# Side work, operand sums and first heads re-ordered in a pipelined attention sweep

## The chip, the cores and the metric

The kernel runs on one core of one Trainium2 chip. The core has five engines with queues of their own: TensorE (PE, matmuls; PEld is its weight load), VectorE (DVE), ScalarE (ACT), GpSimd (POOL) and SyncE (SP, which here only issues DMAs). ACT and POOL issue some DMAs too. Each engine works through its instructions in the order in which they were written into its queue. The metric is the device time of one launch in microseconds (us); lower is better.

## What is computed

One layer of an encoder is applied to two groups of requests, g = 0 and 1, each of 512 tokens of width 1024, with shared weights; all arrays are fp32. A mLSTM branch and an attention branch start from one normalized input and are merged by gates; then come an output projection, a feed-forward block, a gated embedding and a last norm. The change lies in the attention branch. Cut to that:

```
qa = (rmsnorm(c_q, g_q) @ w_uq).reshape(B, S, 8, 128 + 64)
q_nope, q_rope = qa[..., :128], rope(qa[..., 128:], cos, sin)
kv = (rmsnorm(c_kv, g_kv) @ w_ukv).reshape(B, S, 8, 128 + 128)
k_nope, va = kv[..., :128], kv[..., 128:]
k_rope = rope(k_r, cos, sin)
s = q_nope @ k_nope^T + q_rope @ k_rope^T        # per head
p = softmax(s * (128 + 64) ** -0.5)
y_a = (p @ va) @ w_ao
x = x + (g_m * y_m + g_a * y_a) @ w_out          # y_m = (...) @ w_mo, mLSTM branch
```

## The kernel before

**Precision.** An fp32 product is made of three passes on PE: each operand is split into a part rounded for PE ("hi", a cast on ACT) and the rest ("lo", a subtraction on DVE, `lo_of`), and hi·hi, hi·lo and lo·hi are added in PSUM. So each operand costs ACT one instruction and DVE one. The tiles are 128 partitions by 512.

**Order.** Up to the attention sweep, and behind it, the compiler's scheduler simulates the engines and may re-order instructions that do not depend on each other. Within the sweep (`pinned[0]` true, L1121 to L1207) the instructions of PE, ACT, DVE and POOL stand in the order of the source. SP's queue is not pinned, and work written behind the sweep may still be placed among the sweep's.

**Before the sweep** (L701 to L1120). Sixteen merge gates keep PE busy up to 604.8 us. Then come: the split of the latents `lat` (ckv, then cq); the projection of all values (L712: two halves, each 2 groups x 4 blocks x 6 matmuls, written to DRAM as `vd`); the keys' rotary part `kst` (L741: a load `gs`, `rope_steps`, casts `kh`, lo parts `kl`); weights of heads 0 and 1 (`wa_load`, `wa_split`); for head 0 the rotary queries (`rot_proj`, six steps of `rot` on DVE, `rot_hi` on ACT, `rot_lo` on DVE, for both groups), keys and queries (`proj_hi`, `proj_lo`); and the rotary projection of heads 2 and 3, group 0 (`rot_proj(1, 0)`). `rot_proj(m, g)` makes the rotary part for heads 2m and 2m + 1.

**The sweep** (L1122) runs over 17 units u; u = 2 x head + group for 16 of them, and the last only finishes. Four units are a block: m = u // 4, r = u % 4. A unit u does, in this order:

- `score(u, 0)`, `expo(u, 0)`, `score(u, 1)`: five matmuls into a bank, the row maximum on DVE (`mx`), the exponent on ACT (`p`), which also sums the row (`den`);
- the last transposes of the unit before, `turn(u - 1, 3)`: four on PE (`pt`), the hi cast `aph` on ACT, the lo part `apl` on DVE; and the reciprocal `rc` of its row sums on DVE;
- the keys of the next unit (`proj_hi(kn, ...)`, `pj` to `qh`, `ql`), the values' split (`vh` on ACT, `vl` on POOL);
- `sums_row(u - 1)`: `rc` is transposed on PE, copied by ACT into `rb` (one buffer), stored by a DMA of POOL (`rsd`) and read back by another DMA of POOL, spread over 128 partitions;
- **side work**: the operands P1, P2 (r = 1), P7 (r = 2) and P6 (r = 3) of the next stage (`hop_hi`: the sum for P7 on DVE and for P6 on POOL, and the hi casts), and some rotary steps;
- `weigh(u - 1)`: twelve matmuls p · v into `av`; `weighed(u - 1)`: ACT copies it (`oz`), POOL multiplies it by `rb`, and a DMA stores it;
- `turn(u, 0)`, `score(u, 2)`, `turn(u, 1)`, `expo(u, 2)`; then side work again: the weight splits of a later head (r = 1 and 3) and the lo parts of the operands (`los`);
- the queries of the next unit, `score(u, 3)`, `turn(u, 2)`, `expo(u, 3)`; and a `rot_proj` (r = 0 and 3).

At u = 12 the rotary tiles give way to weight tiles of the next stage, and at u = 14 the latents to sixteen tiles X2, into which its operands are then loaded.

**Behind the sweep** two products by 7-multiplication blocks (`chain`, `Seven`, `Ops`) apply w_mo and w_ao. Their operands are sums of quarters, `P1` to `Q4` (`Ops.part`); the sums of the first product, P5 and Q4, are POOL's (L916, L922, L923), and so are most sums of its weights (L975 to L985).

Of the kernel before, what the change touches and what calls it, by code (L numbers as in the profile page):

```python
# [7 lines left out]
F32 = mybir.dt.float32  # L8
F32R = mybir.dt.float32r
# [6 lines left out]
P = 128  # L16
T = 512
NB = T // P
G = 2
# [43 lines left out]
def encoder_kernel(ctx: ExitStack, tc: tile.TileContext, a):  # L63
# [89 lines left out]
    def lo_of(out, src, hi, e=V):  # L153
        e.tensor_tensor(out=out, in0=src, in1=hi.bitcast(F32), op=ALU.subtract)  # L154
# [546 lines left out]
    Q = Slots("Q", vt=2, rb=1, qkv=12, qst=4, p=3, ph=1, pl=1)  # L701
    QL = Slots("QL", lat=16)
    lat = {}
    for n in ("ckv", "cq"):
        lat[n] = [[split(early[f"{n}{i}", g], QL, "lat", n) for i in range(2)] for g in range(G)]

    LAT.close()
# [1 line left out]


    vd = [[dr.tile([NB, P, T], F32, name=f"vd{g}{i}") for i in range(2)] for g in range(G)]
    for half in range(2):  # L712
        whi, wlo = weight(a["wv"][half])
        for g in range(G):
            for i in range(NB):
                bk = bank()
                for k in range(2):
                    n = slice(T * k, T * k + T)
                    hi, lo = (x[:, i * P : (i + 1) * P] for x in lat["ckv"][g][k])
                    E.matmul(bk, hi, whi[:, n], start=k == 0, stop=False)  # L720
                    E.matmul(bk, lo, whi[:, n], start=False, stop=False)
                    E.matmul(bk, hi, wlo[:, n], start=False, stop=k == 1)
# [18 lines left out]
    kst = []  # L741
    for g in range(G):
        gs = AX("rt", "gs")
        nc.sync.dma_start(gs[0:64], gsd[g])
        for _ in rope_steps(gs, AX("rt", "rs"), 2):
            pass
        kh = Q.pool.tile([P, T], F32R, name=f"kh{g}")
        kl = Q.pool.tile([P, T], F32R, name=f"kl{g}")
        for o in (0, 64):
            S.copy(kh[o : o + 64], gs[0:64])  # L750
        for o in (0, 64):
            V.tensor_tensor(out=kl[o : o + 64], in0=gs[0:64], in1=kh[0:64].bitcast(F32), op=ALU.subtract)
        kst.append((kh, kl))

    halves_ = [(hd, g) for hd in range(AH) for g in range(G)]
    NU = len(halves_)
    was, wload, qn, kn, vn, vts, rots, rsteps, qst, att = ({} for _ in range(10))
# [2 lines left out]
        wload[hd] = WP("wst", "wst", F32, (P, 1024))  # L760
        nc.sync.dma_start(wload[hd][:, 0:768], a["wa"][hd])

    def wa_split(hd):
        w = was[hd] = [WP(n, n, F32R, (P, 1024)) for n in ("whi", "wlo")]
        st = wload[hd]
        for c in (slice(256, 768), slice(0, 256)):
            if c.start == 256 or hd in (0, 1, 3, 5):
                S.copy(w[0][:, c], st[:, c])  # L768
                lo_of(w[1][:, c], st[:, c], w[0][:, c])

    def rot_proj(m, g):
        t = rots[m, g] = AX("rt", "rp")
# [319 lines left out]
        srcs = [a["w8"][W8[f"{kind}{i}"]] for i in (c, c + 4)]  # L1092
        return ops, lambda: Seven(srcs, 4, ops, outputs(put), e)

    for hd in range(2):
        wa_load(hd)
        wa_split(hd)
    v_load(0)
    for g in range(G):
        rot_proj(0, g)  # L1100
        rot(0, g, 6)
        rot_hi(0, g)
        rot_lo(0, g)
# [9 lines left out]
    def hop_hi(n, k):  # L1113
        src = hops.part(n, k)
# [3 lines left out]
        return lo, src, hi  # L1118

    hop_load(0)  # L1120
    pinned[0] = True  # L1121
    for u in range(NU + 1):  # L1122
        now, then, nxt = u < NU, u > 0, u + 1 < NU
        m, r = u // 4, u % 4
        if now:
            score(u, 0)
            expo(u, 0)
            score(u, 1)
        if nxt:
            v_load(u + 1)  # L1130
            if r == 0 and m < 3:
                wa_load(2 * m + 2)
            if r == 2 and m < 3:
# [23 lines left out]
        if r == 0 and 0 < m < 4:  # L1157
            rot_hi(m, 1)
            rot_lo(m, 1)
        if m < 3:  # L1160
            if r == 0:
                rot(m + 1, 0, 2)
            if r == 1:
                rot(m + 1, 0, 4)
            if r == 2:
                rot(m + 1, 1, 4)
            if r == 3:
                rot(m + 1, 1, 2)
                rot_hi(m + 1, 0)
                rot_lo(m + 1, 0)  # L1170
# [10 lines left out]
        if r == 1 and m < 3:  # L1181
            wa_split(2 * m + 2)
        if r == 3 and m < 3:
            wa_split(2 * m + 3)
# [12 lines left out]
        if r == 0 and m < 3:  # L1197
# [473 lines left out]
```

## Time and profile before

| what | us |
|---|---|
| three timed runs | 1920.03, 1922.84, 1924.75 (median 1922.84) |
| the profiled execution | 1919.33 |
| its span, first to last instruction | 1917.5 |
| mean granted clock of PE, full speed 1 | 0.985 |
| value projection begins | 604.80 |
| first score matmul | 638.97 |
| first matmul of the next product | 896.16 |

In a row of the timeline stand the start, the length, the engine, the line (all work of the sweep has L79, the helper that pins it, so one goes by names), the operation, out<-in, and in brackets the idle time before it with what ended it. In the table of windows each engine has its busy time and count, then come the granted clock, the DMA engines' share and GB/s. A matmul of 512 columns shows as 0.39 us, but the next starts 0.23 us behind it. A unit is named below by the start of its window.

### The profile page before, as it was taken

How to read it: one execution, taken by the hardware profiler on the slowest of the kernel's cores; microseconds unless marked ns; L12 is line 12 of the kernel's file. 1: busy time of each engine (PE TensorE's matmuls, PEld its weight loads, DVE VectorE, ACT ScalarE, POOL GpSimd, SP SyncE). 2: the span in 40 equal slices, each digit the busy share in tenths (PEclk: the TensorE clock that was granted, in tenths of full speed). 3: DMA queues.
4: the chain of work that ended last, by engine and by line, in shares of the span. 5: the costliest groups of instructions: out<-in, count | busy, mean ns of one | idle time of the engine just before them, and what ended most of it. 6: DMA issues, size and time to landing. Idle time of an engine off the chain costs nothing.

```text
span 1917.5 us, 24414 instructions
## 1 busy us (share of the span) xinstructions
PE 1843.9 (96%) x8817; PEld 1528.6 (80%) x8817; DVE 1240.7 (65%) x2078; ACT 870.7 (45%) x1705; POOL 423.5 (22%) x329
## 2 busy tenths in 40 slices
PE   9999999999999888986999999999999999999997
PEld 7889898988888666764878888888888887878786
DVE  6757576776521777764698578444444469878756
ACT  6355556563323565564353346433333345434432
POOL 0000000100000122245142002566646623011000
PEclk9999999999999999998999999999999999999998
DMA  4211112212324223235664432323222347533242
GB/s 171 62 56 56 66 45 68 65 45 94 121 93 153 87 80 89 78 100 195 211 217 162 134 127 102 105 88 129 94 102 89 116 143 237 169 125 106 95 142 94
DMA packets 102024, 216.10 MB, mean 113 GB/s; under 512 B 11536, under 2 KB 22224, under 8 KB 101904
## 3 DMA queue, kind: packets, MB, share of 16 engines
q1 hardware_dynamic: 87456, 165.49, 25.7%
q10 hardware_dynamic: 12096, 43.00, 6.9%
q0 software_dynamic: 2352, 6.07, 1.1%
q8 instruction: 69, 1.13, 0.3%
q14 instruction: 51, 0.42, 0.1%
HBM read 160.24 MB, written 54.26 MB: 112 GB/s over the span
## 4 chain that ended last, share of the span: by engine, by line
PE 81%; DVE 10%; DMA 3%; ACT 3%; issue 2%; POOL 1%; SPq 0%; ACTq 0%; DVEq 0%; POOLq 0%
PE b L1004 12%; PE b L1006 12%; PE b L1005 12%; PE mm L183 8%; PE mm L185 8%; PE mm L184 8%; PE mm L79 3%; PE nm L622 3%; PE sc L79 2%; PE pj L79 2%; PE mm L542 2%; PE mm L541 2%; PE mm L540 2%; DVE xl L154 1%; PE pt L79 1%
## 5 line engine op out<-in xcount | busy, mean ns | idle before, releaser
L1004 PE MATMUL b<-xh,wp 128*128 128x512 f32 x1148 | 441.4, 392 | 7.2 <-ACT u L1045 2.3
L1005 PE MATMUL b<-xl,wp 128*128 128x512 f32 x1148 | 447.3, 391 | 1.0 <-DVE xl L154 1.0
L1006 PE MATMUL b<-xh,wp 128*128 128x512 f32 x1148 | 443.4, 391 | 0.7 <-DVE wp L154 0.7
L948 ACT CAST wp<-wst 128x512 fp32r<-128x512 f32 (+1 forms) x270 | 164.6, 612 | 303.1 <-PE b L1006 242.5
L154 DVE TENSOR_TENSOR wp<-wst,wp 128x512 fp32r<-128x512 f32 (+1 forms) x270 | 231.6, 860 | 70.0 <-ACT wp L948 69.8
L1004 PEld LDWEIGHTS b<-xh,wp 128*128 128x128 f32 x1148 | 215.5, 188 | 59.4 <-ACT wp L948 6.1
L1005 PEld LDWEIGHTS b<-xl,wp 128*128 128x128 f32 x1148 | 215.5, 188 | 48.3 <-DVE xl L154 2.0
L1006 PEld LDWEIGHTS b<-xh,wp 128*128 128x128 f32 x1148 | 215.5, 188 | 48.2 <-DVE wp L154 1.6
L183 PE MATMUL mm<-hh,whi 128*128 128x512 f32 x560 | 219.3, 392 | 0.0
L184 PE MATMUL mm<-hl,whi 128*128 128x512 f32 x560 | 218.9, 391 | 0.0
L185 PE MATMUL mm<-hh,wlo 128*128 128x512 f32 x560 | 218.8, 391 | 0.0
L1050 DVE TENSOR_TENSOR u<-b,u 128x512 f32<-128x512 f32 x90 | 61.7, 689 | 132.4 <-PE b L1006 82.6
L185 PEld LDWEIGHTS mm<-hh,wlo 128*128 128x128 f32 x560 | 105.4, 188 | 22.0 <-DVE wlo L154 0.3
L183 PEld LDWEIGHTS mm<-hh,whi 128*128 128x128 f32 x560 | 105.6, 189 | 21.6 <-DVE to L382 0.2
L184 PEld LDWEIGHTS mm<-hl,whi 128*128 128x128 f32 x560 | 105.5, 188 | 21.5
L975 POOL TENSOR_TENSOR s<-wst,wst 128x512 f32<-128x512 f32 (+1 forms) x30 | 48.7, 1624 | 319.6 <-DMA wst<-wd 137.5
L168 ACT CAST whi<-wst 128x1024 fp32r<-128x1024 f32 x61 | 64.1, 1051 | 109.5 <-PE mm L184 70.4
L1361 POOL TENSOR_TENSOR sg<-sg,u 128x512 f32<-128x512 f32 x30 | 55.0, 1834 | 204.1 <-DVE u L1050 204.1
L154 DVE TENSOR_TENSOR wlo<-wst,whi 128x1024 fp32r<-128x1024 f32 (+1 forms) x65 | 77.7, 1198 | 34.5 <-ACT whi L768 19.6
L1045 ACT COPY u<-b 128x512 f32<-128x512 f32 x90 | 50.8, 589 | 96.7 <-PE b L1006 69.2
L79 POOL TENSOR_TENSOR vl<-avt,vh 128x512 fp32r<-128x512 f32 x16 | 21.1, 1320 | 307.5 <-ACT vh L79 307.5
L154 DVE TENSOR_TENSOR xl<-ld,xh 128x512 fp32r<-128x512 f32 x105 | 79.2, 785 | 5.0 <-ACT xh L932 4.4
(369 smaller groups left out, 3642.3 us busy)
## 6 DMA issues: line engine op xcount, KB each, us to landing
wst<-w SPq DMA_DIRECT2D x73, 512.0 KB, 3.4
wst<-w ACTq DMA_DIRECT2D x60, 512.0 KB, 3.6
ld<-actd SPq DMA_DIRECT2D x77, 256.0 KB, 3.5
actd<-t SPq DMA_DIRECT2D x40, 256.0 KB, 2.8
x<-x SPq DMA_DIRECT2D x32, 256.0 KB, 4.2
ld<-hzd SPq DMA_DIRECT2D x32, 256.0 KB, 4.3
wst<-wd ACTq DMA_DIRECT2D x16, 512.0 KB, 3.9
actd<-sg SPq DMA_DIRECT2D x30, 256.0 KB, 2.0
```

Of the source, the lines that this page charges most:

```text
L79: r = f(*args, **kw)
L154: e.tensor_tensor(out=out, in0=src, in1=hi.bitcast(F32), op=ALU.subtract)
L168: S.copy(hi[:, :n], st[:, :n])
L183: E.matmul(bk, whi[:, c], hi, start=k == 0, stop=False)
L184: E.matmul(bk, whi[:, c], lo, start=False, stop=False)
L185: last_mm[0] = E.matmul(bk, wlo[:, c], hi, start=False, stop=k == nk - 1)
L622: E.matmul(bk, l, r, start=n == 0, stop=n == len(terms) - 1)
L948: S.copy(hi, src)
L1004: E.matmul(bk, whi[:, c], hi, start=bool(first) and k == 0, stop=False, **sk)
L1005: E.matmul(bk, whi[:, c], lo, start=False, stop=False, **sk)
L1006: E.matmul(bk, wlo[:, c], hi, start=False, stop=k == self.kh - 1, **sk)
L1050: V.tensor_tensor(out=t, in0=b, in1=t, op=ALU.add if name == "P2" else ALU.subtract)
```

## The change

It re-orders; no arithmetic is added or taken away.

1. Before the sweep: cq is split ahead of ckv; head 0's weights, rotary queries, keys and queries and then the keys' rotary part come ahead of the value projection; the values' weights are split into tiles of the pool H in place of the weight pool; head 1's weights are loaded between the two halves and split within unit 0; `rot_proj(1, 0)` moves to the end of unit 0.
2. P6's sum is done at the very start of the units with r = 3, on POOL for m < 3 and on DVE for m = 3; its cast stays where it was, its lo part moves to the next unit.
3. The other side work of DVE and ACT is put singly or by twos between other instructions: P1's and P2's casts ahead of the first exponent, the rotary steps in five places, weight casts and lo parts apart, the lo parts of the operands behind the unit's last lo part. The operands' loads come at r = 0.

```diff
-    for n in ("ckv", "cq"):
+    for n in ("cq", "ckv"):
...
-    for half in range(2):
-        whi, wlo = weight(a["wv"][half])
+    def v_proj(half):
+        st = WP("wst", "wst", F32, (P, 1024))
+        nc.sync.dma_start(st, a["wv"][half])
+        w = [split(st[:, k * T : (k + 1) * T], H, "h", "wv") for k in range(2)]
         for g in range(G):
...
-    def wa_split(hd):
-        w = was[hd] = [WP(n, n, F32R, (P, 1024)) for n in ("whi", "wlo")]
-        st = wload[hd]
-        for c in (slice(256, 768), slice(0, 256)):
-            if c.start == 256 or hd in (0, 1, 3, 5):
-                S.copy(w[0][:, c], st[:, c])
-                lo_of(w[1][:, c], st[:, c], w[0][:, c])
+    QK, RO = slice(256, 768), slice(0, 256)
+    def wa_hi(hd, c):
+        if hd not in was:
+            was[hd] = [WP(n, n, F32R, (P, 1024)) for n in ("whi", "wlo")]
+        S.copy(was[hd][0][:, c], wload[hd][:, c])
+    def wa_lo(hd, c):
+        hi, lo = was[hd]
+        lo_of(lo[:, c], wload[hd][:, c], hi[:, c])
...
-    for hd in range(2):
-        wa_load(hd)
-        wa_split(hd)
-    v_load(0)
+    wa_load(0)
+    wa_split(0, RO)
+    wa_split(0, QK)
     for g in range(G):
         rot_proj(0, g)
+    for to, n, off in ((kn, "ckv", 512), (qn, "cq", 256)):
+        proj_hi(to, 0, n, off)
+        proj_lo(to, 0)
+    for g in range(G):
         rot(0, g, 6)
         rot_hi(0, g)
         rot_lo(0, g)
-    for to, n, off in ((kn, "ckv", 512), (qn, "cq", 256)):
-        proj_hi(to, 0, n, off)
-        proj_lo(to, 0)
-    rot_proj(1, 0)
+    kst = []
...
+    v_proj(0)
+    wa_load(1)
+    v_proj(1)
+    v_load(0)
...
+        if at(3, now):
+            hops.sums = lambda n: V if n == "P7" or m == 3 else GP
+            sub = hops.part("P6", m)
         if now:
             score(u, 0)
+        if at(1):
+            hop_hi("P1", m)
+            hop_hi("P2", m)
+        if at(3, more):
+            rot_hi(m + 1, 0)
         if now:
             expo(u, 0)
             score(u, 1)
...
+        if at(0, 0 < m < 4):
+            rot(m, 1, 1)
+            lo_of(*hlo["P6"])
+            hop_load(m)
+        if at(1, more):
+            rot(m + 1, 0, 1)
+        if at(2):
+            lo_of(*hlo["P2"])
+        if at(3, more):
+            rot_lo(m + 1, 0)
         if then:
             turn(u - 1, 3)
...
             V.reciprocal(out=att[u - 1]["rc"], in_=att[u - 1]["den"])
             turn_lo(u - 1, 3)
+        if at(0, 0 < m < 4):
+            rot(m, 1, 1)
+        if at(1, more):
+            rot(m + 1, 0, 1)
+        if at(2):
+            p7 = hops.part("P7", m)
...
-        los = []
-        if now and r:
-            for n in (("P1", "P2"), ("P7",), ("P6",))[r - 1]:
-                los.append(hop_hi(n, m))
-            if r == 3 and m < 3:
-                hop_load(m + 1)
...
+        if at(0, more):
+            wa_split(2 * m + 1, RO)
+        if at(1, more):
+            rot(m + 1, 0, 2)
+        if at(2):
+            hop_hi("P7", m, p7)
+        if at(2, more):
+            rot(m + 1, 0, 2)
+        if at(3, more):
+            rot(m + 1, 1, 2)
+        if at(3, now):
+            hop_hi("P6", m, sub)
         if then:
             weigh(u - 1)
             weighed(u - 1)
...
-        for x in los:
-            lo_of(*x)
+        if at(0, 0 < m < 4):
+            rot_lo(m, 1)
+        if at(3, more):
+            rot(m + 1, 1, 1)
         if nxt:
             proj_hi(qn, u + 1, "cq", 256)
+        if at(0, m == 0):
+            wa_hi(1, QK)
+        if at(1, more):
+            wa_hi(2 * m + 2, QK)
+        if at(3, more):
+            wa_hi(2 * m + 3, QK)
...
             turn_lo(u, 2)
+        if at(0, m == 0):
+            wa_lo(1, QK)
+        if at(1, more):
+            wa_lo(2 * m + 2, QK)
+        if at(3, more):
+            wa_lo(2 * m + 3, QK)
+        if at(1):
+            lo_of(*hlo["P1"])
+        if at(2):
+            lo_of(*hlo["P7"])
+            if more:
+                rot(m + 1, 1, 1)
+        if at(0, more):
+            rot_proj(m + 1, 0)
+        if at(1, more):
             rot_proj(m + 1, 1)
-        if r == 3 and m < 2:
-            rot_proj(m + 2, 0)
...
+    lo_of(*hlo["P6"])
     pinned[0] = False
```

`at(row, ...)` is true where r is `row` and the further conditions hold; `more` is m < 3; `hop_hi` now keeps the pair for the lo part in `hlo`.

More of the change, by code (lines that the diff above doesn't have):

```diff
@@ L717, in encoder_kernel @@
                 for k in range(2):
-                    n = slice(T * k, T * k + T)
+                    whi, wlo = w[k]
                     hi, lo = (x[:, i * P : (i + 1) * P] for x in lat["ckv"][g][k])
-                    E.matmul(bk, hi, whi[:, n], start=k == 0, stop=False)
-                    E.matmul(bk, lo, whi[:, n], start=False, stop=False)
-                    E.matmul(bk, hi, wlo[:, n], start=False, stop=k == 1)
+                    E.matmul(bk, hi, whi, start=k == 0, stop=False)
+                    E.matmul(bk, lo, whi, start=False, stop=False)
+                    E.matmul(bk, hi, wlo, start=False, stop=k == 1)
                 t = EV(("ch", "bk")[i % 2], "av")
@@ L739, in rope_steps @@
         yield V.tensor_tensor(out=t[0:n], in0=t[0:n], in1=s[0:n], op=ALU.add)
[L741 to L753, printed above, removed]
     halves_ = [(hd, g) for hd in range(AH) for g in range(G)]
@@ L761, in wa_load, with wa_split @@
         nc.sync.dma_start(wload[hd][:, 0:768], a["wa"][hd])
-    def wa_split(hd):
-        w = was[hd] = [WP(n, n, F32R, (P, 1024)) for n in ("whi", "wlo")]
-        st = wload[hd]
-        for c in (slice(256, 768), slice(0, 256)):
-            if c.start == 256 or hd in (0, 1, 3, 5):
-                S.copy(w[0][:, c], st[:, c])
-                lo_of(w[1][:, c], st[:, c], w[0][:, c])
+    QK, RO = slice(256, 768), slice(0, 256)
[6 more added lines that the diff above has]
+        lo_of(lo[:, c], wload[hd][:, c], hi[:, c])
+    def wa_split(hd, c):
+        wa_hi(hd, c)
+        wa_lo(hd, c)
     def rot_proj(m, g):
@@ L1103, in encoder_kernel @@
         rot_lo(0, g)
-    for to, n, off in ((kn, "ckv", 512), (qn, "cq", 256)):
-        proj_hi(to, 0, n, off)
-        proj_lo(to, 0)
-    rot_proj(1, 0)
+    kst = []
+    for g in range(G):
+        gs = AX("rt", "gs")
+        nc.sync.dma_start(gs[0:64], gsd[g])
+        for _ in rope_steps(gs, AX("rt", "rs"), 2):
+            pass
+        kh = Q.pool.tile([P, T], F32R, name=f"kh{g}")
+        kl = Q.pool.tile([P, T], F32R, name=f"kl{g}")
+        for o in (0, 64):
+            S.copy(kh[o : o + 64], gs[0:64])
+        for o in (0, 64):
+            V.tensor_tensor(out=kl[o : o + 64], in0=gs[0:64], in1=kh[0:64].bitcast(F32), op=ALU.subtract)
+        kst.append((kh, kl))
+    v_proj(0)
+    wa_load(1)
+    v_proj(1)
+    v_load(0)
+    hlo = {}
     def hop_load(k):
@@ L1111, in hop_load, with hop_hi @@
             hops.get(x, k)
-    def hop_hi(n, k):
-        src = hops.part(n, k)
+    def hop_hi(n, k, src=None):
+        src = hops.part(n, k) if src is None else src
         hi, lo = op(n, "xh", F32R), op(n, "xl", F32R)
@@ L1117, in hop_hi @@
         hops.x.setdefault(n, []).append((hi, lo))
-        return lo, src, hi
+        hlo[n] = (lo, src, hi)
     hop_load(0)
@@ L1124, in encoder_kernel, with at @@
         m, r = u // 4, u % 4
+        more = m < 3
+        def at(row, *alts):
+            return row == r and all(alts)
+        sub = None
+        if at(3, now):
+            hops.sums = lambda n: V if n == "P7" or m == 3 else GP
+            sub = hops.part("P6", m)
         if now:
             score(u, 0)
+        if at(1):
[3 more added lines that the diff above has]
+            rot_hi(m + 1, 0)
+        if now:
             expo(u, 0)
@@ L1130, in encoder_kernel @@
             v_load(u + 1)
-            if r == 0 and m < 3:
+            if at(0, more):
                 wa_load(2 * m + 2)
-            if r == 2 and m < 3:
+            if at(2, more):
                 wa_load(2 * m + 3)
+        if at(0, 0 < m < 4):
[8 more added lines that the diff above has]
+            rot_lo(m + 1, 0)
         if then:
@@ L1150, in encoder_kernel @@
             sums_row(u - 1)
-        los = []
-        if now and r:
-            for n in (("P1", "P2"), ("P7",), ("P6",))[r - 1]:
-                los.append(hop_hi(n, m))
-            if r == 3 and m < 3:
-                hop_load(m + 1)
-        if r == 0 and 0 < m < 4:
-            rot_hi(m, 1)
[L1159 to L1170, printed above, removed]
+        if at(0, 0 < m < 4):
+            rot_hi(m, 1)
+        if at(0, more):
[4 more added lines that the diff above has]
+            hop_hi("P7", m, p7)
+        if at(2, more):
+            rot(m + 1, 0, 2)
[3 more added lines that the diff above has]
+            hop_hi("P6", m, sub)
         if then:
@@ L1180, in encoder_kernel @@
             turn_lo(u, 1)
[L1181 to L1184, printed above, removed]
-        for x in los:
-            lo_of(*x)
+        if at(0, 0 < m < 4):
+            rot_lo(m, 1)
+        if at(3, more):
+            rot(m + 1, 1, 1)
         if nxt:
             proj_hi(qn, u + 1, "cq", 256)
+        if at(0, m == 0):
[4 more added lines that the diff above has]
+            wa_hi(2 * m + 3, QK)
         if now:
@@ L1196, in encoder_kernel @@
             turn_lo(u, 2)
-        if r == 0 and m < 3:
+        if at(0, m == 0):
[10 more added lines that the diff above has]
+                rot(m + 1, 1, 1)
+        if at(0, more):
+            rot_proj(m + 1, 0)
+        if at(1, more):
             rot_proj(m + 1, 1)
-        if r == 3 and m < 2:
-            rot_proj(m + 2, 0)
         if u == 12:
```

## The prediction

> **What bounds the kernel now.** I read the page first. TensorE (PE) is busy 96% of the span, so the change can only pay where PE stands still or runs at half clock.
>
> ```profile
> span 1917.5 us, 24414 instructions
> ...
> PE   9999999999999888986999999999999999999997
> ...
> PEclk9999999999999999998999999999999999999998
> ```
>
> Each of the 40 slices is 47.9 us. PE falls below 9 in slices 13 to 18 but one (counted from 0), from about 623 us to 911 us, and the clock falls below 9 in slice 18. That is the attention sweep, so next I asked for a table of windows with one row per unit u (from its first score matmul; the first window holds what stands ahead of unit 0, the last holds u = 15 and the tail).
>
> ```profile
> 604.80:638.97 34.17, 30.88 (x128) 24.26 (x127) 13.42 (x21) 15.90 (x28) 0.00 (x0) 0.94 0.62 204
> 638.97:651.95 12.98, 11.53 (x52) 9.17 (x50) 10.58 (x15) 8.19 (x18) 1.28 (x1) 0.89 0.07 20
> 664.50:679.09 14.59, 12.61 (x61) 9.71 (x62) 12.97 (x21) 8.07 (x18) 4.17 (x4) 1.00 0.46 129
> 679.09:699.86 20.77, 15.47 (x69) 12.04 (x68) 13.04 (x21) 11.14 (x25) 6.23 (x6) 0.92 0.26 79
> 740.53:762.74 22.21, 15.57 (x69) 12.10 (x68) 13.14 (x21) 11.24 (x25) 6.18 (x6) 0.89 0.23 70
> 777.12:789.65 12.53, 12.20 (x62) 9.67 (x60) 9.06 (x14) 8.45 (x19) 3.66 (x4) 1.00 0.19 62
> 804.30:822.70 18.40, 13.03 (x64) 10.00 (x62) 10.59 (x16) 9.66 (x21) 6.21 (x6) 0.91 0.24 73
> 862.77:896.16 33.39, 15.98 (x68) 11.68 (x67) 9.30 (x17) 9.10 (x22) 23.06 (x20) 0.74 0.56 197
> sum 257.19, PE 213.06 PEld 165.73 DVE 172.32 ACT 144.44 POOL 87.11; mean PE 13.32 PEld 10.36 DVE 10.77 ACT 9.03 POOL 5.44
> ```
>
> Columns after the length: busy time of PE, PEld, DVE, ACT, POOL, granted clock, DMA share, GB/s. Unit 9 (777.12) shows what PE needs alone: 12.53 us. The units with u mod 4 = 3 (679.09, 740.53, 804.30) take 18.4 to 22.2 us with the clock at 0.89 to 0.92, and the last takes 33.39. Why, the waits, the chain and the timeline of u = 3 say:
>
> ```profile
> ACT xh L79 <- POOL ld L79: 36.2, 4, 15.7
> ...
> 680.46 1.29 POOL L79 TENSOR_TENSOR oz<-oz,rb 128x512 f32<-128x512 f32 x1 [3.21 <-DMA rb<-rsd]
> ...
> 684.90 1.23 POOL vl L79
> 686.13 2.76 DMA rsd<-rb
> ...
> 690.02 1.30 POOL L79 TENSOR_TENSOR ld<-ld,ld 128x512 f32<-128x512 f32 x1
> ...
> 691.36 0.62 ACT L79 CAST xh<-ld 128x512 fp32r<-128x512 f32 x1 [6.38 <-POOL ld L79]
> ...
> 696.42 1.12 PE L79 MATMUL pt<-ident,p 128*128 128x128 f32 x4 [5.30 <-ACT p L79]
> ```
>
> GpSimd (POOL) does vl, issues the store of the row sums (rsd), waits for it to land, issues the load (rb), and only then adds the operand P6 (the 1.30 us `ld<-ld,ld`). ScalarE (ACT) works strictly in order, and its cast of P6 stands ahead of the copies PE needs: it sits 6.38 us, PE 5.30 us. Four such waits are 36.2 us.
>
> **The change, part by part.**
>
> *P6's sum ahead of the transfers.* At u mod 4 = 3 it now stands first in the unit on POOL (on VectorE, DVE, at u = 15). It waits only for P7's lo part, which DVE does at the end of the unit before. In u = 3 POOL can run it behind the previous product's oz, which ends at 681.75, 2.7 us into the unit; so it is done by about 4. The cast stands behind the row sums' copy, some 6 us into the unit: the wait goes. What is late next is vl, by 1.3 us, and nothing wants vl before the next unit. So the three middle units fall from 61.4 us (20.77 + 22.21 + 18.40) towards 12.53 each, half-clock time included.
>
> *Side work singly on DVE.* The units with u mod 4 = 2 lose about 2.0 us each (14.59 less 12.61), because DVE has side work ahead of what PE waits for, as in u = 6:
>
> ```profile
> 726.00 1.28 DVE L79 TENSOR_TENSOR xl<-ld,xh 128x512 fp32r<-128x512 f32 x2
> ...
> 727.80 0.68 DVE L79 TENSOR_TENSOR ql<-pj,qh 128x512 fp32r<-128x512 f32 x1
> ...
> 728.54 0.49 PE L79 MATMUL sc<-qh,ql 128*128 128x512 f32 x1 [1.45 <-DVE ql L79]
> ```
>
> Nothing is removed: the same rotary steps, lo parts and weight splits are spread, one or two in a place. The new places are ahead of the reciprocal and after the unit's last lo part. Their cover is read from u = 3:
>
> ```profile
> 682.50 0.17 DVE L79 RECIPROCAL rc<-den 128x4 f32<-128x4 f32 x1
> ...
> 683.52 0.27 PE L79 MATMUL pt<-ident,rc 128*4 128x128 f32 x1
> ```
>
> The reciprocal is done 0.85 us before PE wants it. A DVE instruction takes 0.6 us from start to start (the two xl above: 1.28), so one ahead of it is free and a second costs about 0.35. Two at the end of a unit also push the next unit's first reduce back. My estimates of PE's stall: 0.4 us in units 0 mod 4 (two ahead), 0.6 in units 2 mod 4 (two behind, one ahead), 1.1 in units 3 mod 4 (two ahead, which meet P6 on POOL), none in 1 mod 4. The meeting is priced from the rows of one group, slower beside POOL's instructions than its 0.6 to 0.7 us alone:
>
> ```profile
> 719.00 2.38 DVE L79 TENSOR_TENSOR rs<-rp,sin 32x512 f32<-32x512 f32 x2
> ...
> 735.10 2.77 DVE L79 TENSOR_TENSOR rs<-rp,sin 32x512 f32<-32x512 f32 x4
> ```
>
> Two in 2.38 against four in 2.77: about 1 us more for one that meets POOL. Bounds of this stall: nothing (6.9 us better than my sum), or in every unit the 2.0 of today's u = 2 (25 worse).
>
> *First heads beside the values' projection.* Today PE runs 96 value matmuls and the 24 of rotary, k and q of head 0 without a pause to 632.95, then waits for DVE's rotary steps:
>
> ```profile
> 629.29 5.57 DVE L737 TENSOR_TENSOR rs<-rp,sin 32x512 f32<-32x512 f32 x8 [0.52 <-ACT rp L773]
> ...
> 632.56 0.39 PE L185 MATMUL pj<-cqh,wlo 128*128 128x512 f32 x1
> 636.24 0.80 PE L183 MATMUL pj<-cqh,whi 128*128 128x512 f32 x1 [3.29 <-DVE ql L154]
> ```
>
> Moved ahead, the 24 come first and DVE's chain (12 rotary steps, 4 lo parts, then 12 instructions for the keys' rotary part: some 19 us at 0.68) runs under 22 us of value matmuls. The last thing score 0 needs (keys of group 0) is, by my count, ready some 10 us early, two 128 KB loads included. The same 120 matmuls need 28.2 us (604.80 to 632.95); I add 1.0 for evictions that meet the casts on ACT. Scores start 29.2 after 604.80 instead of 34.17: 5.0 us gained, from nothing (if the keys' chain lands late) to 6. The rotary projection that stood behind the gap moves into the sweep, where units 0 and 1 mod 4 of the first three groups now carry one each, 1.40 us as the chain shows:
>
> ```profile
> 682.29 1.40 PE pj L79 x6
> ```
>
> *The tail.* At u = 15 POOL also carries sums for the next chain, which the compiler's scheduler put between rsd and rb:
>
> ```profile
> 872.13 0.56 POOL L79 DMA_DIRECT2D rsd<-rb  x1
> ...
> 873.94 3.69 POOL L922 TENSOR_TENSOR ld<-ld,ld 128x512 f32<-128x512 f32 x3
> ...
> 882.46 0.58 POOL L79 DMA_DIRECT2D rb<-rsd  x1
> ...
> 885.95 1.26 POOL L79 TENSOR_TENSOR oz<-oz,rb 128x512 f32<-128x512 f32 x1 [0.41 <-ACT aph L79]
> ...
> 888.14 1.12 PE L79 MATMUL pt<-ident,p 128*128 128x128 f32 x4 [14.49 <-ACT p L79]
> ...
> 901.62 0.39 PE L1004 MATMUL b<-xh,wp 128*128 128x512 f32 x1
> ```
>
> With P6 on DVE, ACT no longer waits here, and PE could reach the next chain 18.3 us after 862.77 (12.53, then 1.4 for the last exponent, 0.6 transposes, 1.0, 2.8 for `weigh`). But POOL's queue stays: ACT's copy of the last row sums needs the one rb buffer, free after oz, which ends 24.4 us after 862.77 and, without P6's 1.3 on POOL, 23. The copy is due at 17.4, so ACT halts some 6 us. PE has two products in hand; the third begins at 901.62, 5.5 us after ACT and PE were both free at 896.16. I take 5 us from ACT's being free, so 28 instead of 18.3 + 5.5: 4.3 us late, with 0.8 for a lower clock. I count 23.4 for 33.39: 10.0 gained; bounds 0 and 15.
>
> *Sum.* Units 0 mod 4: 10.5 for unit 0 (its 11.53 of PE time without the half clock up to 641.72), 12.53 + 1.40 + 0.4 twice, 12.93 in the last group: 52.1. Units 1 mod 4: 13.93 three times and 12.53: 54.3. Units 2 mod 4: 13.13 three times and 12.83: 52.2. Units 3 mod 4: 13.6 three times: 40.8. Tail 23.4. Together 222.8 against 257.2, 34.4 gained; with 5.0 at the start 39.4. The profiled execution took 1919.33 us (1.8 around its span), so 1879.9. The three timed runs have their median at 1922.84, 3.5 above it; the four together average 1921.7, and I put the forecast there: **1882**.
>
> **A rule to weigh: when the clock halves.** The rows, PEclk third from the end:
>
> ```profile
> 631.49:634.90 3.41, 1.45 (x7) 0.88 (x5) 3.31 (x6) 1.18 (x2) 0.00 (x0) 1.00 0.48 166
> 634.90:638.31 3.41, 2.07 (x5) 1.69 (x6) 3.41 (x6) 0.29 (x1) 0.00 (x0) 0.50 0.00 0
> ...
> 689.51:692.92 3.41, 1.61 (x7) 0.97 (x6) 0.40 (x1) 1.54 (x3) 1.80 (x2) 1.00 0.41 95
> 692.92:696.34 3.42, 0.00 (x0) 0.00 (x0) 2.86 (x5) 2.53 (x7) 1.27 (x1) 1.00 0.27 103
> ```
>
> A stretch of 3.41 us in which PE was busy 1.45 was followed by half clock; one with 1.61 was not. So 2 us of standing still, badly placed, is enough, and costs 1.7 us more. [...]
>
> **The rivals.**
> - *The tail's queue decides* (POOL's sums move ahead of vl or rb again, or ACT waits as long elsewhere): the tail gains nothing, 1892. For: POOL is busy 23.06 of 33.39 us there. Against: P6 has left that queue.
> - *All waits go*: stalls nothing, tail 15, start 6: 12.9 more, 1869. Against: the places ahead of the reciprocal.
> - *DVE becomes the bound* in units 2 and 3 mod 4, its instructions each caught by POOL: POOL is busy some 4 us a unit, so at most that much is added to DVE's 10 to 13; 2 us more in six units, 1894. Against: unit 9 has DVE at 9.06 of 12.53.
> - *Slower: the new places halve the clock.* Two instructions stand ahead of a reduce or the reciprocal in most units; if each leaves PE 2.0 us idle in one 3.41 us stretch, every unit pays 2.0 and 1.7. Over 15 units that is 56 us against the 7 in my sum: 1882 + 49 = 1931. It decides from 1.8 us of idle in one stretch. For: 1.45 stood in u = 6. Against: that took three side instructions in a row.
> - *It doesn't do what it says*: the scheduler leaves the start as it is and P6 still waits (for P7's lo part, late on DVE): then 5.0 at the start and 17.8 in units 3 mod 4 (61.4 less 40.8 and two rotary projections) don't come, 1905.
>
> **How the numbers follow.** My forecast 0.52, all waits go 0.12, the tail 0.14, DVE 0.12, slower 0.04, not as it says 0.06. The range takes in the first four with their bounds: 1864 (all waits go, 5 less for the spread of the runs) to 1902 (tail and DVE together would be 1904, less likely than either). Chances about 0.3% (5.8 us, what a measurement here can tell from no change): faster 0.93 (the first four, and half of the last case, as its parts fail one by one), within 0.03 (the other half), slower 0.04.
>
> **What would show it.** Right: no wait of ACT's P6 cast on POOL in u = 3, 7, 11; those units under 14.5 us; no half clock between 640 and 860 us; scores starting about 634; stalls ahead of the reciprocal's transpose of half a microsecond; a stop of ACT in the tail at the row sums' copy. Wrong: a POOL that reaches P6 after vl, gaps of 2 us with clock drops, or a score 0 that waits for the keys' rotary part.

## The result, and the profile after

| | before | after |
|---|---|---|
| timed runs, median | 1922.56 us (1920.03 to 1924.75, 4 runs) | 1903.55 us (1900.27 to 1905.32, 4 runs) |
| ratio, with its 95% interval | | 0.990 (0.988 to 0.992) |
| span of the profiled execution | 1917.5 us | 1898.3 us |

The change is faster by 19 us, 1%. The forecast was 40, and 1903.55 lies just outside the range that ended at 1902. First the head of the page and the slices of PE and its clock, after the change (a slice is 47.5 us):

```profile
span 1898.3 us, 24423 instructions
...
PE   9999999999999999997999999999999999999997
...
PEclk9999999999999999998999999999999999999998
```

The row of eights in PE's slices is gone; slice 18 (854 to 902 us), where the sweep ends, still has a 7, and an 8 of the clock, though PE is through with the sweep at 861.67 now. The table of windows says the same by stages; the columns are those used ahead (length, PE, PEld, DVE, ACT, POOL, granted clock, DMA share, GB/s). The rows are the prologue from the first attention matmul to the first score, units 3, 7, 10 and 11, unit 15 to the end of the sweep, and the stretch behind it:

```profile
605.02:638.80 33.78, 30.20 (x121) 23.12 (x120) 20.61 (x31) 16.59 (x28) 0.00 (x0) 0.95 0.47 160
...
675.22:691.68 16.46, 14.04 (x64) 10.85 (x62) 13.01 (x19) 9.40 (x21) 5.94 (x6) 0.90 0.26 76
731.88:746.75 14.87, 12.44 (x64) 9.70 (x62) 13.02 (x19) 9.41 (x21) 5.38 (x5) 1.00 0.28 84
774.86:786.79 11.93, 11.93 (x62) 9.74 (x61) 9.74 (x16) 7.42 (x17) 3.92 (x4) 1.00 0.46 148
786.79:801.67 14.88, 12.45 (x64) 9.70 (x63) 13.24 (x19) 9.41 (x21) 5.43 (x5) 1.00 0.21 65
840.04:861.67 21.63, 17.37 (x70) 12.81 (x69) 13.66 (x18) 8.75 (x21) 18.25 (x16) 0.84 0.64 227
861.67:896.30 34.63, 23.20 (x100) 18.77 (x99) 15.90 (x24) 13.13 (x26) 11.61 (x7) 0.88 0.58 197
```

The prologue takes 33.78 us, nearly its old 34.17. Units 3, 7 and 11 have come down from 20.77, 22.21 and 18.40, and unit 10 is PE alone. Unit 15 is 11.8 us shorter, but in the 34.63 us behind the sweep PE works for only 23.20. Laid out along the span:

| stretch | before | after | gain | forecast |
|---|---|---|---|---|
| end of the merge gates to the first score | 34.17 | 33.78 | 0.4 | 5.0 |
| first score to the start of unit 15 | 223.80 | 201.24 | 22.6 | 24.4 |
| start of unit 15 to the last instruction | 1054.68 | 1058.28 | -3.6 | 10.0 |

(The first stretch began 0.22 us later, so the span fell by 19.1 to 19.2.) The middle came nearly as forecast. The start's gain is missing, and the tail's has turned into a loss.

**Start.** The timeline of the changed kernel, VectorE's rows and then PE's:

```profile
607.20 5.58 DVE L741 TENSOR_TENSOR rs<-rp,sin 32x512 f32<-32x512 f32 x8 [1.29 <-ACT rp L770]
612.81 0.69 DVE L154 TENSOR_TENSOR ql<-pj,qh 128x512 fp32r<-128x512 f32 x1
...
614.02 0.68 DVE L154 TENSOR_TENSOR ql<-pj,qh 128x512 fp32r<-128x512 f32 x1
...
613.56 0.50 PE L723 MATMUL mm<-wvh,ckvh 128*128 128x512 f32 x1 [2.93 <-DVE ql L154]
```

and two stretches of the table of windows:

```profile
611.51:614.92 3.41, 1.36 (x6) 1.12 (x7) 3.36 (x6) 0.00 (x0) 0.00 (x0) 1.00 0.00 0
614.92:618.33 3.41, 3.41 (x9) 2.31 (x8) 2.95 (x5) 2.32 (x4) 0.00 (x0) 0.50 0.13 38
```

The keys and queries of head 0 lie in two PSUM banks until their lo parts `ql` have read them, and the value projection needs banks. But `ql` stands on DVE behind eight rotary steps, 5.58 us. So PE waits 2.93 us, up to 613.56, and half clock follows from 614.92 to 618.33.

**Units 3, 7, 11.** No ACT instruction waits for P6 any more. What is left, in unit 3:

```profile
677.58 1.66 DVE L79 TENSOR_TENSOR rs<-rp,sin 32x512 f32<-32x512 f32 x1
679.26 1.29 DVE L79 TENSOR_REDUCE mx<-sc 128x1 f32<-128x512 f32 x2
680.58 1.39 DVE L79 TENSOR_TENSOR qs<-rp,qs 64x512 fp32r<-64x512 f32 x2
681.98 0.18 DVE L79 RECIPROCAL rc<-den 128x4 f32<-128x4 f32 x1
...
682.31 0.27 PE L79 MATMUL pt<-ident,rc 128*4 128x128 f32 x1 [2.42 <-DVE rc L79]
```

A rotary step that meets POOL takes 1.66 us instead of 0.7 (so in units 3 and 7; in unit 11 it is the `xl` ahead of it that takes 1.66), both row maxima follow it, then two lo parts of the rotary queries, and only then the reciprocal. PE waits 2.42 us in each of the three units, where 1.1 was forecast, and in unit 3 half clock comes on top.

**Tail.** POOL, ACT, DVE, SP and PE from unit 15 on (SPq and ACTq rows are the issuing of DMAs):

```profile
852.76 3.72 POOL L919 TENSOR_TENSOR ld<-ld,ld 128x512 f32<-128x512 f32 x3
...
861.97 1.30 POOL L920 TENSOR_TENSOR ld<-ld,ld 128x512 f32<-128x512 f32 x1
864.81 1.29 POOL L79 TENSOR_TENSOR oz<-oz,rb 128x512 f32<-128x512 f32 x1 [1.53 <-DMA rb<-rsd]
...
866.13 0.25 ACT L79 COPY rb<-pt 4x128 f32<-4x128 f32 x1 [9.12 <-POOL oz L79]
...
872.94 6.35 POOL L79 TENSOR_TENSOR oz<-oz,rb 128x512 f32<-128x512 f32 x1 [3.34 <-DMA rb<-rsd]
...
872.64 1.89 DVE L154 TENSOR_TENSOR xl<-ld,xh 128x512 fp32r<-128x512 f32 x3
...
875.05 2.49 DVE L154 TENSOR_TENSOR xl<-ld,xh 128x512 fp32r<-128x512 f32 x4
...
879.32 0.32 SPq L873 DMA_DIRECT2D ozd<-oz  x1
...
888.10 0.33 ACTq L958 DMA_DIRECT2D wst<-w  x1
888.47 0.62 ACT L929 CAST xh<-ld 128x512 fp32r<-128x512 f32 x1 [12.83 <-DMA ld<-ozd]
...
894.30 0.62 ACT L945 CAST wp<-wst 128x512 fp32r<-128x512 f32 x1 [4.21 <-DMA wst<-w]
...
894.97 0.80 PE L1001 MATMUL b<-xh,wp 128*128 128x512 f32 x1 [11.43 <-ACT wp L945]
```

Read it from the top. POOL's operand sums stand between the two transfers of unit 14's row sums, so its oz comes at 864.81. ACT has waited 9.12 us for that, because the copy of unit 15's row sums needs the one `rb` buffer. The last oz therefore starts at 872.94, and then takes 6.35 us instead of 1.29, beside a run of DVE's `xl` subtractions. Only behind it go the store and the loads at the end of which ACT stands 12.83 us. The next weights' load is one that ACT issues itself, so it starts only at 888.10, and its cast waits for it up to 894.30: PE stops for 11.43 us. In the kernel before the last oz took 1.29 us:

```profile
899.82 1.29 POOL L79 TENSOR_TENSOR oz<-oz,rb 128x512 f32<-128x512 f32 x1 [2.92 <-ACT u L1045]
```

It ended 38.34 us behind the start of unit 15; now the last oz ends 39.25 behind it, though PE is through the sweep 12 us sooner.

### The profile page after: what moved, and what is told of

It is laid out like the page before. It is cut to its first block, busy times and chain, and to the rows that moved or that the text cites. A ratio compares the mean times of both kernels' runs of the same rounds, so it can differ in the third digit from the quotient of the medians.

```text
span 1898.3 us, 24423 instructions
## 1 busy us (share of the span) xinstructions
PE 1841.2 (97%) x8817; PEld 1526.5 (80%) x8817; DVE 1241.7 (65%) x2081; ACT 867.5 (46%) x1707; POOL 420.2 (22%) x328
## 4 chain that ended last, share of the span: by engine, by line
PE 45%; DVE 5%; DMA 2%; issue 2%; POOL 1%; ACT 1%; ACTq 0%; SPq 0%; DVEq 0%; POOLq 0%
PE b L1001 12%; PE b L1003 12%; PE b L1002 12%; PE mm L79 2%; PE mm L185 1%; PE mm L184 1%; PE mm L183 1%; DVE xl L154 1%; PE mm L1521 1%; PE mm L1519 1%; PE mm L1520 1%; DVE wp L154 1%; DMA ld<-ozd 1%; POOL oz L79 0%; DMA rb<-rsd 0%
## 5 line engine op out<-in xcount | busy, mean ns | idle before, releaser
L154 DVE TENSOR_TENSOR wlo<-wst,whi 128x1024 fp32r<-128x1024 f32 (+2 forms) x61 | 74.2, 1217 | 14.6 <-ACT whi L168 13.4
```

## The experiments

Theory at the outset: three causes, one for each stretch (the lo parts behind the rotary steps; the side work ahead of the reciprocal; POOL's sums among its transfers). The rivals: the loads behind the sweep are held by SP's order; the middle's gain is due to the dealing out and not to P6. "Middle" is the stretch from the first score to unit 15. "The kernel before" stands beside each group of runs at 1920.8 to 1922.2 us.

**1. The lo parts first.** The change, with keys and queries of head 0 ahead of the rotary products:

```diff
-    for g in range(G):
-        rot_proj(0, g)
     for to, n, off in ((kn, "ckv", 512), (qn, "cq", 256)):
         proj_hi(to, 0, n, off)
         proj_lo(to, 0)
+    for g in range(G):
+        rot_proj(0, g)
```

> The changed kernel, with head 0's keys and queries projected ahead of its rotary queries, so that DVE does their two lo parts ahead of the rotary steps. Theory (the value projection's first matmul waits for a PSUM bank, and the bank for a lo part that stands behind 5.6 us of rotary steps on DVE): the 2.9 us wait of PE at 613.6 us and the half clock from 614.9 go, the first score starts at about 634 us in place of 638.8, and as all behind it moves along, the time falls by 4 to 5 us against the changed kernel (about 1899). Rival (evictions on ACT or the keys' rotary chain set the start anyway): the first score stays within 1.5 us of 638.8 and the time within 2 us of 1903.

1897.32 us (1894.62 to 1901.13), ratio 0.9875 (0.9858 to 0.9892). Its windows row for the prologue:

```profile
606.50:636.48 29.98, 28.15 (x122) 22.25 (x120) 20.82 (x31) 16.29 (x28) 0.00 (x0) 1.00 0.55 180
```

and in its timeline the first value matmul, with no bracket, so no wait:

```profile
612.32 0.39 PE L723 MATMUL mm<-wvh,ckvh 128*128 128x512 f32 x1
```

No half clock (1.00 in the row), and 29.98 us instead of 33.78: 3.8 gained, 0.8 short of the 29.2 forecast. (The first score stands at 636.48 and not at 634. Counted from the start of the span it says less, since executions differ in what comes before: the prologue begins at 604.80 us in the kernel before, at 605.02 in the change and at 606.50 here.)

**2. The sums behind the sweep on VectorE.** All twelve:

```diff
     hops.raw = lambda g, k: load(hzd[g][k], X2, "x")
+    hops.sums = lambda n: V
```

> The changed kernel, with the twelve operand sums for P5 and Q4 of the first product behind the sweep on DVE in place of POOL. Theory (the end of the sweep is set by POOL's queue: twelve sums of 1.26 us between the last two heads' row sums, so that the last oz is stored 17.7 us after PE has left the sweep, and SP, ACT and PE wait in turn): the last multiply of oz ends some 10 us or more sooner against the start of u = 15, the 11.4 us wait of PE about 33 us behind the sweep falls below 3 us, and the time falls by 9 to 14 us against the changed kernel. Rival 1 (the loads of the next product's operands are late by themselves, sixteen tiles of 256 KB at once): the wait keeps over 8 us, the time moves less than 3 us. Rival 2 (DVE, with 7 us more in u = 15, becomes the bound): PE waits for DVE instead, over 6 us in u = 15.

1890.41 us (1882.66 to 1892.98), ratio 0.9827 (0.98 to 0.9854). The tail of its timeline:

```profile
862.00 1.27 POOL L79 TENSOR_TENSOR oz<-oz,rb 128x512 f32<-128x512 f32 x1 [3.02 <-ACT p L79]
...
863.30 0.26 ACT L79 COPY rb<-pt 4x128 f32<-4x128 f32 x1 [0.68 <-POOL oz L79]
...
871.42 1.60 POOL L79 TENSOR_TENSOR oz<-oz,rb 128x512 f32<-128x512 f32 x1 [3.05 <-ACT wp L945]
...
849.42 0.27 PE L79 MATMUL pt<-ident,rc 128*4 128x128 f32 x1 [3.95 <-DVE rc L79]
```

ACT's 9.12 us are 0.68, the last oz ends 30.84 us behind unit 15 and not 39.25, the stop of 11.43 is gone, and unit 15 to the last instruction is 1047.34: 10.9 less than in the change. The last row is the price: two sums stand on DVE ahead of row maxima and of unit 14's reciprocal, and PE waits 3.95 us for that where it waited 1.80 in the change.

**3. The last store from POOL,** so that nothing on SP's queue stands behind it:

```diff
-        nc.sync.dma_start(ozd[g][hd], o)
+        (GP if u == NU - 1 else nc.sync).dma_start(ozd[g][hd], o)
```

> The changed kernel, with the store of the last head's output (one DMA) issued by POOL, behind its multiply, in place of SP. It tells whether the loads behind the sweep are late because SP's queue stands behind that one store. If SP's order is what passes POOL's lateness on: the loads of ozd 4 to 7 are issued near 869 us in place of 882, the 11.4 us wait of PE falls to under 3 us, and the time falls by 8 to 11 us. If the loads truly need the late data, or tiles that come free late: the wait stays above 8 us and the time within 2 us of the changed kernel.

1901.16 us (1900.49 to 1902.78), ratio 0.9895 (0.988 to 0.991): no different from the change.

```profile
868.76 12.03 SPq L877 DMA_DIRECT2D ld<-tad  x4
...
894.90 0.80 PE L1001 MATMUL b<-xh,wp 128*128 128x512 f32 x1 [12.87 <-ACT wp L945]
```

SP now takes 12.03 us over four loads of `tad`, which the sweep doesn't write, and gets through them only when the last oz has ended. So the store ahead of the loads in SP's queue is not the cause: the loads wait for the oz by themselves. As their data are not the sweep's, it is probably the place they are loaded into that comes free late; no run tests that.

**4. P6 alone.** The kernel before, with P6's subtraction (one in each unit r = 3) issued at the start of these units and nothing else:

```diff
+        if now and r == 3:
+            hops.sums = lambda n: V if n == "P7" or m == 3 else GP
+            sub = hops.part("P6", m)
         if now:
             score(u, 0)
...
-                los.append(hop_hi(n, m))
+                los.append(hop_hi(n, m, sub if n == "P6" else None))
```

> The kernel before, with P6's sum alone moved to the start of the units 3 mod 4 (POOL for the first three, DVE for the last, as in the change); start and side work as before. Theory (this wait carries the gain in the middle of the sweep): the units at 679, 741 and 804 us fall from 61.4 us together to about 43, the time from the first score to the start of u = 15 falls by 16 to 20 us, the time behind the start of u = 15 falls by less than 4 us as POOL's queue keeps it, and the time is 14 to 20 us under the kernel before, about that of the changed kernel. Rival (dealing out the side work gave the gain, or is needed for it): the middle falls by less than 10 us.

1895.68 us (1893.36 to 1897.24), ratio 0.9864 (0.9849 to 0.9879). Middle 203.41, 20.4 of the change's 22.6. One edit, and it is 7.9 us faster than the whole change; here the last oz ends 34.76 us behind unit 15. Of the change's 22.6, 2.4 are unit 0's (10.56 us for 12.98), which the new start brings to full clock. In the units behind it P6 alone gains 20.6 and the whole change, with one rotary projection more in the sweep, 20.1.

**5. All but P6.** The change with P6's sum back behind POOL's transfers (the edit of run 4 taken out).

> The change with one edit taken back: the two subtractions that make the sixth operand (P6) are again issued where the kernel before has them, behind the POOL transfers of the row sums; the rest of the change stays. Theory A (P6's place on POOL is what carried the middle, as it did when it was moved alone): units 3, 7 and 11 get their long idle stretch back, and the stretch from the first score to the start of unit 15 goes from 201.2 us back to some 217 to 222, the time by about +16 to +20, so a median near 1920. Rival B (the other side work that was dealt out singly carries a good part of the middle): the stretch stays under 212 and the time under 1914.

1910.85 us (1908.32 to 1914.09), ratio 0.9945 (0.9926 to 0.9965). The waits of this kernel between 638 and 838 us, columns total, times, longest:

```profile
ACT xh L79 <- POOL ld L79: 19.3, 3, 6.8
PE pt L79 <- ACT p L79: 9.5, 4, 4.1
```

The same of the kernel before:

```profile
ACT xh L79 <- POOL ld L79: 20.6, 3, 7.7
PE pt L79 <- ACT p L79: 20.5, 7, 6.6
```

Middle 212.33: neither as forecast by theory A (217 to 222) nor quite under 212 as by its rival, whose time (under 1914) did come. ACT stands as long for P6 as before, 19.3 us for 20.6, but PE pays only 9.5 us for it, where it paid 20.5. So the rest of the change does carry something: 11.5 us alone (2.4 of them in unit 0, by the new start), against 20.4 for P6 alone and 22.6 for both. They cover the same loss, and do not add.

**6. The reciprocal first.** The change, with the lo parts of the rotary queries behind the reciprocal, and the rotary step from the end of r = 2 in r = 3's group:

```diff
-        if at(3, more):
-            rot_lo(m + 1, 0)
         if then:
             turn(u - 1, 3)
...
         if at(2):
             p7 = hops.part("P7", m)
+        if at(3, more):
+            rot_lo(m + 1, 0)
...
         if at(3, more):
-            rot(m + 1, 1, 2)
+            rot(m + 1, 1, 3)
...
         if at(2):
             lo_of(*hlo["P7"])
-            if more:
-                rot(m + 1, 1, 1)
```

> The change with the rotary side work of the third and fourth heads of each group put elsewhere: the two low parts rot_lo(m+1,0) stand behind the reciprocal and not ahead of the row maximum, and the rotary step at the end of r 2 goes to the group of r 3. Theory A (the idle 2.42 us of PE ahead of the transposes in units 3, 7 and 11 is DVE's row maximum and reciprocal standing behind these): the idle falls to 0.2 to 1.0 in each of the three, the stretch from the first score to unit 15 from 201.2 to 195 to 198, and the half clock at 683 us goes; time 1897 to 1900. Rival B (the wait is for P6's two subtractions on POOL and the oz ahead of them, and DVE only shares it): the idle stays above 1.8 each and the stretch within 1 us of 201.2. Behind unit 15 nothing changes (1058 within 2 us).

1894.39 us (1892.22 to 1896.85), ratio 0.9858 (0.9833 to 0.9884). Its units 3 and 7:

```profile
674.88:687.19 12.31, 12.30 (x65) 9.76 (x63) 11.43 (x19) 9.07 (x21) 5.16 (x5) 1.00 0.28 86
727.47:739.78 12.31, 12.30 (x65) 9.76 (x63) 11.43 (x19) 9.09 (x21) 4.60 (x4) 1.00 0.29 86
```

The idle is gone altogether, more than expected. Middle 193.15, 8.1 less: three times 2.4 and the half clock at 683, less a wait in unit 8 that is 0.9 longer. Two things were moved at once here, and no run tells which of them did it.

**7. Eight of the twelve sums on VectorE,** P5's four left on POOL:

```diff
     hops.raw = lambda g, k: load(hzd[g][k], X2, "x")
+    hops.sums = lambda n: GP if n == "P5" else V
```

> The change with eight of the twelve operand sums behind the sweep (those of Q4) on VectorE, while P5's four stay on POOL. Theory A (the transfers of unit 14's and 15's row sums stand behind POOL's sums, and the last oz with them): the last oz multiply ends 30 to 33 us behind the start of unit 15, where the change has 39.25 and all twelve on VectorE 30.84; the idle 11 us of PE near 895 goes; unit 15 to the last instruction 1044 to 1049; and since no sum stands ahead of unit 14's row maximum now, unit 15 starts within 0.5 us of the change's 201.24 behind the first score, not 203.29. Time 1887 to 1892. Rival B (a sum on VectorE costs there what it saves on POOL): the last oz is early, but the time stays within 3 us of the change's 1903.5.

1894.79 us (1892.56 to 1896.88), ratio 0.986 (0.9834 to 0.9885). The last oz ends 32.74 us behind unit 15, the stop at 895 is gone, and unit 15 is not late (middle 201.61). That unit 15 came later in run 2, 203.29, is mostly not the sums' effect: there unit 11 fell into half clock, 16.47 us for the change's 14.88. Unit 15 to the last instruction is 1052.29 here and not under 1049, and the time lies outside the 1887 to 1892 of theory A and behind that of run 2: freeing POOL halfway gave 6.0 of the 10.9.

**8. Three edits together:** runs 1, 6 and 7.

> The change with three edits together: the projections of the first heads ahead of the rotary products (so that the low parts that release PSUM come first on VectorE), Q4's eight sums on VectorE, and the rotary side work of the fourth head of each group moved behind the reciprocal. If the three causes are separate and on the path one after the other, the gains add: 3.8 (start, by the length of the prologue) + 11 (tail) + 4 (middle) off 1903.5, so 1883 to 1887. Rival: they overlap (what the start or the middle gains is only waited for behind the sweep), and the time stays at 1889 to 1893, that of the tail's edit alone.

1878.07 us (1875.89 to 1880.71), ratio 0.9774 (0.9749 to 0.9799). Prologue 29.99, middle 193.71, tail 1050.13. Against the change's 1903.55 the three edits gained 6.2, 9.2 and 8.8 one by one, and 25.5 together. The time is shorter even than the 1883 to 1887 expected, and as the runs of one kernel spread over 4 to 7 us here, which edit gave more than its price cannot be said. But the gains add, so the three causes are separate and lie one behind the other on the path.

**9. All twelve, with the other two edits:** runs 1, 6 and 2.

> The change with the projections of the first heads first, the rotary side work of the fourth head of each group moved behind the reciprocal, and all twelve operand sums behind the sweep on VectorE (the run before this one had eight of them there and gave 1878.1). If the tail goes by the last oz alone: it ends 1.5 to 2 us earlier from the start of unit 15 than with eight, but two sums stand ahead of unit 14's row maximum again and cost unit 15 some 2 us of PE, so 1876 to 1880, the same within its interval. Rival (the tail is worth more when POOL is quite free, as the two runs with the tail's edit alone had 1890.4 against 1894.8): 1872 to 1876.

1878.13 us (1876.88 to 1881.95), ratio 0.9778 (0.9765 to 0.9791): the same as run 8. The last oz ends 31.15 us behind unit 15, 1.2 sooner than in run 8, and the tail is 1.5 us shorter (1048.61), but the time doesn't show it; the rival's 1872 to 1876 did not come.

**10. Two of P5's four on POOL,** ten sums on VectorE, with runs 1 and 6:

```diff
+    two = iter((GP, GP))
+    hops.sums = lambda n: next(two, V)
```

> As the run with all twelve sums on VectorE, but the first two of P5's four stay on POOL, where they come before its transfers have anything to wait for, so that no sum stands ahead of unit 14's row maximum on VectorE. Expected: unit 15's idle ahead of the transposes 1.8 us and not 3.9, the last oz 31 to 32.5 us behind the start of unit 15, time 1872 to 1877, the shortest of all. Rival: the time equals that with eight within 1.5 us (1878), because what is left of the tail is the row sums' way through DRAM and not POOL or VectorE.

1882.36 us (1876.08 to 1884.32), ratio 0.9791 (0.9774 to 0.9808). The wait ahead of unit 15's transposes is 1.80, as expected, the last oz ends at 30.81, a little sooner than expected, and this kernel has the shortest profiled span (1874.3); but its other runs are 4.9 to 8.2 us longer than that one, and the median is outside the 1872 to 1877 and no gain. Runs 8 to 10 cannot be told apart.

**11. The kernel before with two edits:** P6 early (run 4) and the twelve sums on VectorE (run 2).

> The kernel before with two edits only: the P6 subtractions ahead of the transfers on POOL, and all twelve operand sums behind the sweep on VectorE; start and the rest of the side work as before. It asks what is left for the dealing out and the new start. P6's place alone gave 1895.7. If the tail's edit is worth here what it is worth in the change (13 us), the time is 1882 to 1885; if POOL's sums were no burden where the sweep ends on the old order (rival: the last oz of the P6 run already ended 34.8 us behind unit 15, of which 31 can be had), it is 1889 to 1893. Middle 203 to 205.5 us in both.

1892.45 us (1890.85 to 1893.5), ratio 0.9848 (0.9834 to 0.9861). The rival was right: behind the old order the tail's edit is worth only some 3 us on top of run 4. Dealing out and new start, once mended, are worth the other 14.

**12. The last oz on VectorE,** a single execution:

```diff
-        GP.tensor_tensor(out=o, in0=o, in1=x["rb"], op=ALU.mult)
+        (V if u == NU - 1 else GP).tensor_tensor(out=o, in0=o, in1=x["rb"], op=ALU.mult)
```

> The change with the last multiplication oz (unit 15's) on VectorE, all else the same. It asks what the 6.35 us that this multiplication took on POOL beside VectorE's subtractions cost, where 1.29 is usual. Theory A (the loads behind it wait for it, so its length is on the path): its store and the loads come some 5 us earlier against its operand's arrival, and the idle 11.4 us of PE near 895 falls to 5 to 7. But VectorE works in order and will stand at it until the row sums land, so PE stands ahead of the P6 product instead, some 4 to 8 us; the whole within 4 us of the change. Rival B (the loads wait for something else): the idle near 895 stays at 10 to 12 and the time gets longer by 4 to 8 us.

1900.87 us. DVE and PE in its timeline:

```profile
878.30 0.69 DVE L79 TENSOR_TENSOR oz<-oz,rb 128x512 f32<-128x512 f32 x1 [16.28 <-DMA rb<-rsd]
...
879.64 0.50 PE L1002 MATMUL b<-xl,wp 128*128 128x512 f32 x1 [3.23 <-DVE xl L79]
...
896.03 0.50 PE L1001 MATMUL b<-xh,wp 128*128 128x512 f32 x1 [2.95 <-ACT wp L945]
```

DVE, in order, stands 16.28 us in front of it, and PE pays 3.23 and 1.18 us there; but the stop near 896 is 2.95 instead of 11.43. About half of these 8.5 us is only that PE gets there later. Against the start of unit 15 the matmul behind the stop comes 2.9 us sooner (52.02 for 54.93), as the oz ends 4.3 us sooner (34.98 for 39.25), and unit 15 to the last instruction is 1055.1 for 1058.28. So the length of the last oz was on the path, and is worth some 3 us of the tail.

## Why the prediction missed, and what of it held

- **What bounds, and P6's wait: right.** ACT's wait for P6 is gone from units 3, 7 and 11 (runs 4 and 5 show it from both sides).
- **The middle: near in the sum, 22.6 for 24.4, by two errors that cancel in part, which is luck.** Units with r = 2 came better than forecast (48.9 for 52.2 in all), those with r = 3 worse (46.2 for 40.8). The step "1.1 in units 3 mod 4 (two ahead, which meet P6 on POOL)" was mis-sized: it priced one instruction meeting POOL, but DVE also had both row maxima in between. The stretched step, two maxima and two lo parts come one behind the other ahead of the reciprocal, PE waits 2.42 us, and run 6 got all of it back by changing that order.
- **The start: the step that failed is "Moved ahead, the 24 come first and DVE's chain ... runs under 22 us of value matmuls".** It counted when DVE's results are wanted by the scores, but not what they release. `ql` frees the PSUM bank that the next value matmul writes, so the first thing to be late was a bank at 613.56, not an operand at 634. 2.93 us of waiting and 1.7 of half clock make the 4.6 between 33.78 and 29.2; run 1, which has neither, recovered 3.8.
- **The tail: the step that failed is its sum, which ended at the third product.** The cause was named: ACT halts at the copy of the row sums, behind POOL's oz (6 us forecast, 9.12 measured). Up to the next product the tail even came better than forecast, 21.63 us for 23.4. But PE had enough in hand to go on until 883; the price is paid where the loads that wait for the last oz are used, and this was not followed: a stop of 11.43 us, and half clock from 887.97 to 898.21. With POOL's sums moved away the tail gains 7.3 (run 2) of the 10.0. The bounds "0 and 15" did not allow for a loss, and no term of the sum allowed for an oz of 6.35 us. Not all of the loss of 3.6 is here, though. Counted in the two traces, the 301st matmul of the next product starts 103.15 us behind the start of unit 15 for 101.88 before: 1.3 lost. The other 2.3 are lost farther behind, and no run says to what.
- **The rivals.** "The tail's queue decides" (1892, chance 0.14) was the nearest by mechanism, and still 11.6 us short, because the start failed as well and the tail lost. "It doesn't do what it says" has the nearest number, 1905, but P6's wait, of which it was made, had gone: that is luck. The range allowed for one rival at a time.
- **Its own signs.** Of the signs of being right, P6's wait and ACT's stop in the tail came as written; the units under 14.5 us, the full clock from 640 to 860 us, the scores at 634 and stalls of half a microsecond did not. Gaps of 2 us, named as a sign of being wrong, came in units 3, 7 and 11, one of them with a clock drop.
- **When the clock halved.** After the change the stretch from 679.78 to 683.19 again had PE busy for a part, 0.99 of 3.41 us, and the next was at half clock (as at the start, where 1.36 stood ahead of it):

```profile
679.78:683.19 3.41, 0.99 (x6) 0.78 (x6) 3.35 (x7) 3.14 (x9) 0.73 (x2) 1.00 0.41 128
683.19:686.60 3.41, 3.41 (x10) 2.64 (x9) 2.34 (x3) 0.43 (x1) 1.65 (x2) 0.50 0.26 77
```

  So the 2.42 us of unit 3 cost 4.15 there, and 2.56 and 2.43 in units 7 and 11, which kept their clock (1.00 in their rows, 0.90 in unit 3's), against the 12.31, 12.31 and 12.45 of run 6. Which unit pays was not the same in every profile: unit 7 alone took 16.39 us in run 1, units 3 and 7 took 16.45 and 16.62 in run 3, and all three took 16.3 to 16.6 in run 12. So a middle read from one profile is uncertain by about 1.6 us for each such unit.

Mended in its three places, the change takes 1878 us, close to the 1882 forecast, but by other shares: run 8 has 193.71 in the middle where 199.4 was forecast, and 1050.13 in the tail where it was 1044.7. What the change was to bring is there to be had; the forecast missed what its own moves put in front of it.

What stays open: where the tail's other 2.3 us go; how the 10.9 us of run 2's tail divide between the sums ahead of unit 14's transfers and the stretched last oz, of which run 12 prices only the second, at some 3; and why executions of run 10 spread over 8 us.

## What to carry to other kernels

When work is moved on an engine, ask not only who wants its result but also what its reading frees: here a PSUM bank given back late stopped the value projection for 2.93 us, up to 613.56, while the first score came at 638.80, and the one `rb` buffer stopped ACT for 9.12 us. POOL looked idle, busy for 11.61 of the 34.63 us behind the sweep, and still the last release hung on it, so follow a tail to the last load that waits, and not to the first matmul that starts. And undo and do each part alone: here one of the parts was faster than all of them, and the three faults added up cleanly.

## What the runs showed of the hardware

Beside the other's work, an instruction of POOL or DVE could take much longer here than alone. POOL's oz (128x512, 1.29 us for the one before it) took 6.35 us beside DVE's subtractions, and it ended at 879.29, 1.15 us behind the end of their run at 878.14, so about its own length behind it. It works the other way too: a DVE subtraction of 0.68 us stood beside a run of POOL's sums for 6.18 us in the change (from 857.65, and the run ended at 863.27), and for 10.48 us in run 4:

```profile
854.82 10.48 DVE L79 TENSOR_TENSOR xl<-ld,xh 128x512 fp32r<-128x512 f32 x1
```

It is not always so. In unit 3 of the change the rotary step, from 677.58 to 679.24, ended 0.55 us behind the first of two POOL instructions that follow each other at once, and the second then took 1.72 us:

```profile
677.30 1.39 POOL L79 TENSOR_TENSOR oz<-oz,rb 128x512 f32<-128x512 f32 x1 [3.16 <-ACT qs L79]
678.65 1.72 POOL L79 TENSOR_TENSOR ld<-ld,ld 128x512 f32<-128x512 f32 x1
```

So in unit 3 the delay was about that of one instruction; in the tail it was about that of the other engine's whole run, and the delayed instructions took 6.18 to 10.48 us. What decides between the two, no run here shows.
